# Transforming a long filter with half the rows: taps turned in pairs by half an angle, the skip term moved into tap 0, and 21 weight low parts made by an adding transfer

## The chip, the core and the metric

The kernel runs on one core of a Trainium2 chip. A core has a matrix engine, TensorE (PE in the profile; PEld is its loading of weights), and three engines for everything else: VectorE (DVE), ScalarE (ACT) and GpSimd (POOL). SyncE (SP), ScalarE and GpSimd also issue DMA transfers. Each engine works through its own queue in order, and an instruction waits there until the semaphores that it needs have arrived. The metric is the device time of one execution in microseconds, the median of several runs.

## What is computed

One layer of an encoder on 512 tokens of width 2048: a normalised input is projected; one branch is a Hyena convolution with long two-sided filters (1024 channels), the other an attention; both are gated, added and projected, and a SwiGLU network follows. All is float32. The change touches the Hyena branch alone:

```python
def implicit_filter(...):                 # h: a small network over 512 positions
    h_fwd = h[:, :HYENA_W] * decay
    h_bwd = h[:, HYENA_W:] * decay
    k = jnp.concatenate([h_fwd, jnp.zeros((1, HYENA_W)), h_bwd[:0:-1]], axis=0)
    return k / jnp.sum(jnp.abs(k), axis=0, keepdims=True)

def bidir_fft_conv(u, k):
    uf = jnp.fft.rfft(u, n=2 * L, axis=1)
    kf = jnp.fft.rfft(k, n=2 * L, axis=0)
    return jnp.fft.irfft(uf * kf[None], n=2 * L, axis=1)[:, :L]

    z = hv * x1
    z = bidir_fft_conv(z, filt) + hy_bias * z
    y_h = z * x0
```

The term `hy_bias * z` is called the skip term below. It equals a filter whose tap 0 is larger by `hy_bias`.

## The kernel before

**Products in three parts.** Every float32 operand of a matmul is cut into a high part (rounded, `fp32r`) and a low part (what is left). A product is three matmuls: high by high, high by low, low by high (`mm3`). A group of 512 output columns is one matmul row of 128 x 512.

**Weights.** All weight matrices lie in DRAM as one array `wpk` of tiles of 128 x 1024, in the order of use. `wblk` (L173) hands them out in blocks of 128 columns, 8 to a tile. For each tile SP loads `raw` (two buffers), ScalarE copies it to the high part `wh` and VectorE subtracts to get the low part `wl` (three buffers each; L186 to L188). Tiles 16 to 71 do that with priority, so they stand early in each queue. One block feeds one `mm3` of a projection, 24 matmuls for a tile.

**The Hyena stage** lasts from about 20 to 400 us. The 1024 channels go in four quarters `q` of 256, two tiles of 128 channels each. TensorE runs the projections `px` and `phv` (for `x1`, `hv` and `x0`) without end, and generators put the filter and the convolution between their matmuls: each `yield n` means "go on n steps later", where a step is one block of a projection (three matmuls). They are:

- `taps_gen(q)` (L355): the filter network's last product, times decay, gives forward and backward taps `fd`, `bd`; their absolute sum gives the norm `rn`; `hs`, `hd` are sums and differences of both, even and odd positions apart.
- `filter_gen(q)` (L390): transposes `hs` and `hd` (`ktp`, 16 transposes), splits them into high and low parts (`k...h`, `k...l`), and multiplies them with tables of cosines and sines `CS` of 256 x 256 in two parts (`kp`). The tables are cut in halves of 128 frequencies, `fb` 0 and 1, and 128 taps, `j` 0 and 1. The results are turned by an angle per frequency (`cosw`, `sinw`) into three factors `K` and written to DRAM, to `kd[q]` (POOL's queue).
- `conv_gen(q)` (L435): transposes the signal (`ztp`, split into `zt...h` and `zt...l`), multiplies it with the same tables (`up`), loads the factors back (`kc`, two buffers, POOL's queue), forms the complex products on VectorE (`cu`, `cv`, `Y`), splits them, and transforms back (`ab`). It scales by `rn`, adds the skip term (L504) and multiplies by `x0`.

For each quarter the order is: projections, `conv_gen(q)` queued, `filter_gen(q + 1)` queued; `taps_gen(q + 1)` runs inside `conv_gen(q)`. A scheduler puts the instructions of each engine into one fixed order when the kernel is built. Filter work shares seven buffers (`work`, L286) and eight banks of PSUM.

After this stage come attention, gates, output projection and the feed-forward network, which the change leaves as they are.

Of the kernel before, what the change touches and what calls it, by code (L numbers as in the profile page):

```python
# [11 lines left out]
F32 = mybir.dt.float32  # L12
# [5 lines left out]
P = 128  # L18
S = 512
# [34 lines left out]
W_FIRST = 16, 72  # L54

# [4 lines left out]
for _name, _w in (("mixg", KT), ("ffng", KT), ("bgate", 2 * KT), ("cw", 72), ("cb", 24), ("hyb", HT),  # L60
                  ("cosw", 2), ("sinw", 2), ("nsinw", 2), ("one", 1)):
    PC[_name] = _n
    _n += _w
# [50 lines left out]
def layer_kernel(tc, wpk, xT, par, flt, zemb, w4, decT, tb2, rope, qkg, out):  # L114
# [13 lines left out]
    def ps_tile(name):  # L128
        return banks["pool"].tile([P, S], F32, tag="ps", bufs=banks["n"], name=name)
# [43 lines left out]
    def wblk(nb=1):  # L173
        st = state
        if st["pos"] >= BLK:
            i = st["tile"]
            raw = wpool.tile([P, BLK * P], F32, tag="raw", bufs=2, name=f"wr{i}")
            hi = wpool.tile([P, BLK * P], F32R, tag="whi", bufs=3, name=f"wh{i}")
            lo = wpool.tile([P, BLK * P], F32R, tag="wlo", bufs=3, name=f"wl{i}")
            st.update(tile=i + 1, pos=0, hi=hi, lo=lo, raw=raw)  # L180

        i, n = st["tile"] - 1, {1: XW // 2, 2: XW}.get(st["tile"], BLK)
        if st["pos"] % n == 0:
            c = slice(st["pos"] * P, (st["pos"] + n) * P)
            with tc.high_priority() if W_FIRST[0] <= i < W_FIRST[1] else nullcontext():
                nc.sync.dma_start(st["raw"][:, c], wpk[i, :, c])  # L186
                nc.scalar.copy(st["hi"][:, c], st["raw"][:, c])  # L187
                nc.vector.tensor_tensor(st["lo"][:, c], st["raw"][:, c], st["hi"][:, c].bitcast(F32), ALU.subtract)  # L188
# [43 lines left out]
    prm = cpool.tile([P, NPC + 6], F32, name="prm")[:, :NPC]  # L232
# [53 lines left out]
    def work(name):  # L286
        return cw(name, [P, S], "wk", 7)
# [67 lines left out]
    def taps_gen(q):  # L355
# [3 lines left out]
        for c in range(2):  # L359
# [17 lines left out]
            nc.vector.tensor_tensor(r, n2[:, 0:1], n2[:, 1:2], ALU.add)  # L377
            nc.vector.tensor_scalar(r, r, 256.0, None, ALU.mult)
# [11 lines left out]
    def filter_gen(q):  # L390
# [17 lines left out]
        kd[q] = dpool.tile([256, 6 * 256], F32, tag=f"kd{q}", bufs=1, name=f"kd{q}")  # L408
        for fb in range(2):
            g = []  # L410
            for i in range(2):
                kp = ps_tile(f"kp{q}{fb}{i}")
                for j in range(2):
# [5 lines left out]
            nc.scalar.activation(cr, g[0], AF.Copy, scale=pcol("cosw", fb))  # L419
            nc.scalar.activation(ci, g[1], AF.Copy, scale=pcol("cosw", fb))  # L420
            k1, k2, k3 = (work(f"K{i}{q}{fb}") for i in range(3))
            nc.vector.scalar_tensor_tensor(k1, g[1], pcol("sinw", fb), cr, ALU.mult, ALU.add)
            nc.vector.scalar_tensor_tensor(k2, g[0], pcol("nsinw", fb), ci, ALU.mult, ALU.add)
            nc.vector.scalar_tensor_tensor(k3[:, :256], g[1][:, 256:], pcol("nsinw", fb), cr[:, 256:], ALU.mult, ALU.add)
            nc.vector.scalar_tensor_tensor(k3[:, 256:], g[0][:, 256:], pcol("sinw", fb), ci[:, 256:], ALU.mult, ALU.add)
            rows = kd[q][fb * P:(fb + 1) * P]
# [8 lines left out]
    def conv_gen(q):  # L435
# [61 lines left out]
        for c in range(2):  # L497
# [6 lines left out]
            nc.vector.scalar_tensor_tensor(y, zl[c], pcol("hyb", ct), y, ALU.mult, ALU.add)  # L504
# [844 lines left out]
def _constants():  # L1349
# [33 lines left out]
    return tb2, cosw, sinw, zemb, decT, rope  # L1383


def _arrays(inp):
# [3 lines left out]
    tb2, cosw, sinw, zemb, decT, rope = _constants()  # L1390
# [27 lines left out]
    put("one", np.ones((P, 1), f4))  # L1418

# [28 lines left out]
```

## Time and profile before

| | us |
|---|---|
| median of 3 runs (2510.12 to 2510.76) | 2510.73 |
| the profiled execution | 2510.3 |
| its span, first to last instruction | 2508.5 |
| of which VectorE is busy | 2071.2 |
| of which ScalarE is busy | 1180.0 |

The profile holds one execution. A row of its time line gives the start in us, the duration, the engine, the line of the source, the operation with output and inputs, and in square brackets how long the engine stood idle before and who released it. A row may merge several equal instructions (x2). Matmuls overlap, so the time that one costs is the distance from its start to the next one's start. VectorE and ScalarE rows overlap by about 0.1 us in the same way. In the table of DMA issues the last number is the median time from issue to landing. "Waits" lists who waited for whom, with the total, how often, and the longest.

### The profile page before, as it was taken

How to read it: one execution, taken by the hardware profiler on the slowest of the kernel's cores; microseconds unless marked ns; L12 is line 12 of the kernel's file. 1: busy time of each engine (PE TensorE's matmuls, PEld its weight loads, DVE VectorE, ACT ScalarE, POOL GpSimd, SP SyncE). 2: the span in 40 equal slices, each digit the busy share in tenths (PEclk: the TensorE clock that was granted, in tenths of full speed). 3: DMA queues.
4: the chain of work that ended last, by engine and by line, in shares of the span. 5: the costliest groups of instructions: out<-in, count | busy, mean ns of one | idle time of the engine just before them, and what ended most of it. 6: DMA issues, size and time to landing. Idle time of an engine off the chain costs nothing.

```text
span 2508.5 us, 34437 instructions
## 1 busy us (share of the span) xinstructions
PE 2501.2 (100%) x13162; PEld 2150.4 (86%) x13162; DVE 2071.2 (83%) x2936; ACT 1180.0 (47%) x1755; POOL 177.5 (7%) x287
## 2 busy tenths in 40 slices
PE   9999999999999999999999999999999999999999
PEld 7888888888888888888888888888888888888888
DVE  7799974855579999664999999999999988997988
ACT  6434324554455445443544444444444455445443
POOL 0000002020000000000000000000000002001111
PEclk9999999999999999999999999999999999999999
DMA  6344443223554444554333333333333348557754
GB/s 214 109 137 134 133 145 108 71 97 117 178 176 155 143 154 144 185 176 140 112 117 120 132 112 126 118 121 132 110 134 110 132 137 214 151 146 189 193 154 109
DMA packets 113281, 350.41 MB, mean 140 GB/s; under 512 B 13723, under 2 KB 15003, under 8 KB 112892
## 3 DMA queue, kind: packets, MB, share of 16 engines
q1 hardware_dynamic: 70128, 248.02, 29.8%
q0 software_dynamic: 22576, 63.19, 9.6%
q10 hardware_dynamic: 20412, 37.00, 4.8%
q8 instruction: 103, 1.69, 0.3%
q14 instruction: 62, 0.51, 0.1%
HBM read 297.56 MB, written 54.26 MB: 140 GB/s over the span
## 4 chain that ended last, share of the span: by engine, by line
PE 80%; DVE 1%; ACT 0%; issue 0%; ACTq 0%
PE fx L132 19%; PE fy L132 10%; PE b L132 7%; PE o L132 7%; PE gx L132 6%; PE d L132 5%; PE fz L132 5%; PE dx L132 4%; PE ex L132 3%; PE gy L132 3%; PE dy L132 2%; PE ey L132 2%; PE gz L132 2%; PE q L132 1%; PE dz L132 1%; PE av L132 1%
## 5 line engine op out<-in xcount | busy, mean ns | idle before, releaser
L187 ACT CAST wh<-wr 128x1024 fp32r<-128x1024 f32 (+1 forms) x168 | 173.2, 1031 | 289.3 <-PE o L132 65.9
L188 DVE TENSOR_TENSOR wl<-wr,wh 128x1024 fp32r<-128x1024 f32 (+1 forms) x168 | 201.1, 1197 | 123.0 <-ACT wh L187 122.0
L881 ACT CAST fwhs<-fs 128x1024 fp32r<-128x1024 f32 x176 | 184.7, 1050 | 87.3 <-PE fz L132 68.9
L883 DVE TENSOR_TENSOR fwls<-fs,fwhs 128x1024 fp32r<-128x1024 f32 x176 | 214.6, 1219 | 4.4 <-ACT fwhs L881 4.3
L881 ACT CAST fwha<-fa 128x1024 fp32r<-128x1024 f32 x132 | 138.9, 1053 | 151.5 <-PE fx L132 83.8
L132 PE MATMUL px<-xh,wh 128*128 128x512 f32 x576 | 180.5, 395 | 0.0
L132 PE MATMUL fx<-fX,fwhs 128*128 128x512 f32 x704 | 175.3, 391 | 0.6 <-DVE fv L925 0.6
L132 PE MATMUL fy<-fX,fwhs 128*128 128x512 f32 x704 | 175.4, 391 | 0.0
L132 PE MATMUL fx<-fX,fwha 128*128 128x512 f32 x704 | 172.0, 391 | 0.2 <-DVE c L930 0.2
L883 DVE TENSOR_TENSOR fwla<-fa,fwha 128x1024 fp32r<-128x1024 f32 x132 | 161.4, 1223 | 10.0 <-ACT fwha L881 9.8
L132 PE MATMUL o<-ms,wh 128*128 128x512 f32 x512 | 157.8, 389 | 0.0
L132 PEld LDWEIGHTS fx<-fX,fwhs 128*128 128x128 f32 x704 | 129.3, 188 | 25.7 <-DVE fv L925 0.9
L132 PEld LDWEIGHTS fx<-fX,fwha 128*128 128x128 f32 x704 | 129.3, 188 | 25.4 <-issue 0.6
L132 PEld LDWEIGHTS fy<-fX,fwhs 128*128 128x128 f32 x704 | 129.3, 188 | 24.9
L132 PEld LDWEIGHTS px<-xh,wh 128*128 128x128 f32 x576 | 106.7, 189 | 24.1 <-issue 2.4
L132 PE MATMUL d<-act,wh 128*128 128x512 f32 x384 | 118.3, 389 | 0.0
L132 PEld LDWEIGHTS o<-ms,wh 128*128 128x128 f32 x512 | 96.1, 188 | 19.9
L132 PE MATMUL px<-xh,wl 128*128 128x512 f32 x288 | 113.0, 392 | 0.0
L874 DVE TENSOR_TENSOR fs<-fa,fa 128x1024 f32<-128x1024 f32 x88 | 107.2, 1219 | 1.7 <-PE o L132 1.0
L874 DVE TENSOR_TENSOR fs<-fs,fa 128x1024 f32<-128x1024 f32 x88 | 107.3, 1219 | 1.0 <-PE o L132 0.2
L132 PE MATMUL o<-ms,wl 128*128 128x512 f32 x256 | 99.7, 389 | 0.0
L132 PE MATMUL fy<-fX,fwls 128*128 128x256 f32 x704 | 98.7, 283 | 0.0
(965 smaller groups left out, 5891.0 us busy)
## 6 DMA issues: line engine op xcount, KB each, us to landing
fa<-wpk SPq DMA_DIRECT2D x176, 512.0 KB, 3.9
wr<-wpk SPq DMA_DIRECT2D x162, 512.0 KB, 3.5
ga<-wpk SPq DMA_DIRECT2D x60, 512.0 KB, 3.7
da<-wpk SPq DMA_DIRECT2D x32, 512.0 KB, 3.8
ea<-wpk SPq DMA_DIRECT2D x32, 512.0 KB, 4.2
actd<-c POOLq DMA_DIRECT2D x41, 256.0 KB, 4.2
actr<-actd ACTq DMA_DIRECT2D x41, 256.0 KB, 4.1
kc<-kd POOLq DMA_DIRECT2D x16, 512.0 KB, 4.4
```

Source lines behind the costliest of these rows:

```text
L132: tc.keep_in_program_order(nc.tensor.matmul(out, lhsT=lhsT, rhs=rhs, start=start, stop=stop, **kw))
L187: nc.scalar.copy(st["hi"][:, c], st["raw"][:, c])
L188: nc.vector.tensor_tensor(st["lo"][:, c], st["raw"][:, c], st["hi"][:, c].bitcast(F32), ALU.subtract)
L874: raws["sum"] = nc.vector.tensor_tensor(t, a, b, ALU.add).ins
L881: nc.scalar.copy(hi, w)
L883: raws["wl"] = nc.vector.tensor_tensor(lo, w, hi.bitcast(F32), ALU.subtract).ins
```

## The change

**Half the rows.** The taps belong to a transform with an odd frequency grid. If each tap and its mirror in the upper half are first turned by half an angle, every frequency of the even half is the sum, and every one of the odd half the difference, of the same two results, and these come from one table of 128 x 128 in place of 256 x 256. So `hs` and `hd` are laid out with the upper half mirrored, the transposed taps are turned (`kt`, `kr`, with `cosa`, `sina`) before they are split, and each product `kp` uses one block of the table. The two results of a sum are combined by one more step (`kc` copy and `G`; `inner` masks the first row) into the values of both halves. The halves `fb` are now even and odd frequencies, so the rows of `kd` alternate, and the loads of the second half start one row later and fetch the last row apart (127 rows and 1 row).

**The skip term** is added to tap 0 (one column, times the filter's norm), and the line that added it to the result is gone.

**Low parts by transfer.** For the 21 even tiles from 8 to 48 the low part is no longer VectorE's subtraction. ScalarE writes the negated, rounded tile into `wl`, and a DMA of POOL's queue reads the same tile from DRAM again and adds it.

```diff
+W_FETCH = range(8, 50, 2)
...
                 nc.scalar.copy(st["hi"][:, c], st["raw"][:, c])
-                nc.vector.tensor_tensor(st["lo"][:, c], st["raw"][:, c], st["hi"][:, c].bitcast(F32), ALU.subtract)
+                if i in W_FETCH:
+                    nc.scalar.activation(st["lo"][:, c], st["raw"][:, c], AF.Copy, scale=-1.0)
+                    nc.gpsimd.dma_start(st["lo"][:, c], wpk[i, :, c], accum_op=ALU.add)
+                else:
+                    nc.vector.tensor_tensor(st["lo"][:, c], st["raw"][:, c], st["hi"][:, c].bitcast(F32), ALU.subtract)
...
+            nc.vector.scalar_tensor_tensor(fd[:, :1], r, pcol("hyb", 2 * q + c), fd[:, :1], ALU.mult, ALU.add)
...
+            ahead = fd.rearrange("p (m n) -> p n m", n=2)
+            back = bd[:, 1:].rearrange("p (m n) -> p n m", n=2)[:, ::-1]
             for h, op in ((hs, ALU.add), (hd, ALU.subtract)):
-                nc.vector.tensor_tensor(h[:, :256], fd[:, ::2], bd[:, 2::2], op)
-                nc.vector.tensor_tensor(h[:, 256:], fd[:, 1::2], bd[:, 1:S:2], op)
+                h = h.rearrange("p (n m) -> p n m", n=2)
+                nc.vector.tensor_tensor(h[:, :, :P], ahead[:, :, :P], back[:, :, :P], op)
+                nc.vector.tensor_tensor(h[:, :, P:][:, :, ::-1], ahead[:, :, P:], back[:, :, P:], op)
...
-                taps.append(split(cv, tp, "kh", "kl", 4, 4, f"k{i}{q}{j}"))
+            for j in range(2):
+                t = tmp(f"kt{q}{i}{j}")
+                nc.scalar.activation(t, tps[1 - j], AF.Copy, scale=pcol("sina" if i == j else "nsina"))
+                turned = work(f"kr{q}{i}{j}")
+                nc.vector.scalar_tensor_tensor(turned, tps[j], pcol("cosa"), t, ALU.mult, ALU.add)
+                taps.append(split(cv, turned, "kh", "kl", 4, 4, f"k{i}{q}{j}"))
             yield 3
...
+        for i in range(2):
+            g = [ps_tile(f"kp{q}{i}{w}") for w in range(2)]
+            for w in range(2):
+                mm3(g[w], part(w, 0, 3 * P, 4 * P), part(w, 1, 3 * P, 4 * P), *taps[2 * i + (w ^ i)], True, True)
+            cc = tmp(f"kc{q}{i}")
+            nc.scalar.copy(cc, g[0])
+            for fb, (a, b, op) in enumerate(((g[1], cc, ALU.add), (cc, g[1], ALU.subtract))):
+                spectra[fb].append(work(f"G{q}{fb}{i}"))
+                nc.vector.scalar_tensor_tensor(spectra[fb][i], a, pcol("inner"), b, ALU.mult, op)
+            yield 3
         for fb in range(2):
-            g = []
-            for i in range(2):
-                kp = ps_tile(f"kp{q}{fb}{i}")
-                for j in range(2):
-                    a = j * 256 + fb * P
-                    mm3(kp, part(i, 0, a, a + P), part(i, 1, a, a + P), *taps[2 * i + j], j == 0, j == 1)
-                g.append(kp)
-                yield 2
+            g = spectra[fb]
...
-            rows = kd[q][fb * P:(fb + 1) * P]
+            rows = kd[q].rearrange("(p s) c -> p s c", s=2)[:, 1 - fb]
...
-                nc.gpsimd.dma_start(kc[ph], kd[q][fb * P:(fb + 1) * P, ph * S:ph * S + 2 * S])
+                for p0, r0, n in ((0, 129, P - 1), (P - 1, 0, 1)) if fb else ((0, 1, P),):
+                    nc.gpsimd.dma_start(kc[ph][p0:p0 + n], kd[q][r0:r0 + n, ph * S:ph * S + 2 * S])
...
-            nc.vector.scalar_tensor_tensor(y, zl[c], pcol("hyb", ct), y, ALU.mult, ALU.add)
```

The order in which the instructions stand moves in three places that matter. A row names the line, the operation, output, inputs and shape.

First VectorE's queue in the first quarter, from the filter's factors `K` to the first low part of the transposed signal, `zt00l`, which the convolution's matmul `up000` reads. Before:

```order
L422 SCALAR_TENSOR_TENSOR K000_1073<-kp001_1056,prm_78,kcr00_1069 128x512
L423 SCALAR_TENSOR_TENSOR K100_1074<-kp000_1043,prm_78,kci00_1070 128x512
L424 SCALAR_TENSOR_TENSOR K200_1075<-kp001_1056,prm_78,kcr00_1069 128x256
L188 TENSOR_TENSOR wl20_1234<-wr20_1232,wh20_1233 128x1024
L425 SCALAR_TENSOR_TENSOR K200_1075<-kp000_1043,prm_78,kci00_1070 128x256
L558 TENSOR_TENSOR x13u_1091<-px13_970,rbc_542 128x512
L422 SCALAR_TENSOR_TENSOR K001_1126<-kp011_1109,prm_78,kcr01_1122 128x512
L423 SCALAR_TENSOR_TENSOR K101_1127<-kp010_1083,prm_78,kci01_1123 128x512
L424 SCALAR_TENSOR_TENSOR K201_1128<-kp011_1109,prm_78,kcr01_1122 128x256
L425 SCALAR_TENSOR_TENSOR K201_1128<-kp010_1083,prm_78,kci01_1123 128x256
L209 TENSOR_TENSOR zt00l_1145<-ztp00_1139,zt00h_1144 128x512
```

And now, from the third of the factors on (K000 and K100 stand just ahead):

```order
L444 SCALAR_TENSOR_TENSOR K200_1132<-G001_1099,prm_78,kcr00_1126 128x256
L445 SCALAR_TENSOR_TENSOR K200_1132<-G000_1076,prm_78,kci00_1127 128x256
L442 SCALAR_TENSOR_TENSOR K001_1144<-G011_1101,prm_78,kcr01_1140 128x512
L443 SCALAR_TENSOR_TENSOR K101_1145<-G010_1078,prm_78,kci01_1141 128x512
L580 SCALAR_TENSOR_TENSOR hvo2_973<-hv2u_974,prm_78,hvo2_973 128x511
L444 SCALAR_TENSOR_TENSOR K201_1146<-G011_1101,prm_78,kcr01_1140 128x256
L581 SCALAR_TENSOR_TENSOR hvo2_973<-hv2u_974,prm_78,hvo2_973 128x511
L194 TENSOR_TENSOR wl21_1327<-wr21_1325,wh21_1326 128x1024
L600 TENSOR_TENSOR z2_979<-hvo2_973,x1o2_860 128x512
L445 SCALAR_TENSOR_TENSOR K201_1146<-G010_1078,prm_78,kci01_1141 128x256
L604 TENSOR_TENSOR zf2_981<-z2_979 128x256 x2
L215 TENSOR_TENSOR zt00l_1163<-ztp00_1157,zt00h_1162 128x512
```

Before, the factors of the first half were made while the matmuls of the second half ran; now both sets follow the last of the matmuls, and the short convolution `hvo2`, a weight low part and `z2`, `zf2` have come to stand ahead of `zt00l`.

Second ScalarE's queue at the same place, now: `wl20` is the negated copy for the adding transfer, `kcr` and `kci` are what the factors `K` wait for. Before, a single weight copy stood ahead of each pair.

```order
L430 COPY kc01_1097<-kp010_1089 128x512
L189 CAST wh20_1269<-wr20_1268 128x1024
L191 ACTIVATE wl20_1270<-wr20_1268 128x1024
L439 ACTIVATE kcr00_1126<-G000_1076,prm_78 128x512
L440 ACTIVATE kci00_1127<-G001_1099,prm_78 128x512
L439 ACTIVATE kcr01_1140<-G010_1078,prm_78 128x512
L214 CAST zt00h_1162<-ztp00_1157 128x512
L440 ACTIVATE kci01_1141<-G011_1101,prm_78 128x512
```

So `kcr00` comes behind two copies of a whole weight tile, and all four of `kcr` and `kci` stand after the last spectrum matmul.

Third VectorE's queue at the taps of the second quarter. Before, the low parts of the taps follow the skip term (L504) and the last products of the quarter before:

```order
L504 SCALAR_TENSOR_TENSOR y1_1565<-z1_678,prm_78,y1_1565 128x512
L209 TENSOR_TENSOR k010l_1582<-ktp100_1576,k010h_1581 128x512
L508 TENSOR_TENSOR yh1_750<-yh1_750,y1_1565 128x512
L188 TENSOR_TENSOR wl28_1779<-wr28_1777,wh28_1778 128x1024
L209 TENSOR_TENSOR k011l_1591<-ktp101_1585,k011h_1590 128x512
L209 TENSOR_TENSOR k110l_1609<-ktp110_1603,k110h_1608 128x512
L209 TENSOR_TENSOR k111l_1618<-ktp111_1612,k111h_1617 128x512
```

Now the turnings `kr` stand among them:

```order
L415 SCALAR_TENSOR_TENSOR kr100_1611<-ktp100_1599,prm_78,kt100_1609 128x512
L528 TENSOR_TENSOR yh1_752<-yh1_752,y1_1583 128x512
L377 MEMSET bd20_2008 128x1
L215 TENSOR_TENSOR k010l_1614<-kr100_1611,k010h_1613 128x512
L415 SCALAR_TENSOR_TENSOR kr101_1619<-ktp101_1600,prm_78,kt101_1617 128x512
L415 SCALAR_TENSOR_TENSOR kr110_1646<-ktp110_1634,prm_78,kt110_1644 128x512
L215 TENSOR_TENSOR k011l_1622<-kr101_1619,k011h_1621 128x512
L215 TENSOR_TENSOR k110l_1649<-kr110_1646,k110h_1648 128x512
```

The weight low part `wl28` is gone from this place, since tile 28 is one of the 21, and three turnings stand ahead of `k011l`.

More of the change, by code (lines that the diff above doesn't have):

```diff
@@ L60 @@
 for _name, _w in (("mixg", KT), ("ffng", KT), ("bgate", 2 * KT), ("cw", 72), ("cb", 24), ("hyb", HT),
-                  ("cosw", 2), ("sinw", 2), ("nsinw", 2), ("one", 1)):
+                  ("cosw", 2), ("sinw", 2), ("nsinw", 2), ("one", 1),
+                  ("cosa", 1), ("sina", 1), ("nsina", 1), ("ncosw", 1), ("inner", 1)):
     PC[_name] = _n
@@ L229, in rsqrt @@
         return y
-    prm = cpool.tile([P, NPC + 6], F32, name="prm")[:, :NPC]
+    prm = cpool.tile([P, NPC + 1], F32, name="prm")[:, :NPC]
     nc.scalar.dma_start(prm, par)
@@ L395, in filter_gen @@
         for i, src in enumerate((hs_l, hd_l)):
-            for j in range(2):
-                tp = ps_tile(f"ktp{q}{i}{j}")
+            tps = [ps_tile(f"ktp{q}{i}{j}") for j in range(2)]
+            for j, tp in enumerate(tps):
                 for n in range(4):
@@ L408, in filter_gen @@
         kd[q] = dpool.tile([256, 6 * 256], F32, tag=f"kd{q}", bufs=1, name=f"kd{q}")
-        for fb in range(2):
-            g = []
-            for i in range(2):
-                kp = ps_tile(f"kp{q}{fb}{i}")
-                for j in range(2):
-                    a = j * 256 + fb * P
-                    mm3(kp, part(i, 0, a, a + P), part(i, 1, a, a + P), *taps[2 * i + j], j == 0, j == 1)
-                g.append(kp)
-                yield 2
+        spectra = [], []
+        for i in range(2):
[8 more added lines that the diff above has]
+            yield 3
+        for fb in range(2):
+            g = spectra[fb]
+            sin, nsin = ("sinw", "nsinw")[::1 - 2 * fb]
             cr, ci = tmp(f"kcr{q}{fb}"), tmp(f"kci{q}{fb}")
             nc.scalar.activation(cr, g[0], AF.Copy, scale=pcol("cosw", fb))
-            nc.scalar.activation(ci, g[1], AF.Copy, scale=pcol("cosw", fb))
+            nc.scalar.activation(ci, g[1], AF.Copy, scale=pcol("ncosw" if fb else "cosw"))
             k1, k2, k3 = (work(f"K{i}{q}{fb}") for i in range(3))
-            nc.vector.scalar_tensor_tensor(k1, g[1], pcol("sinw", fb), cr, ALU.mult, ALU.add)
+            nc.vector.scalar_tensor_tensor(k1, g[1], pcol(sin, fb), cr, ALU.mult, ALU.add)
             nc.vector.scalar_tensor_tensor(k2, g[0], pcol("nsinw", fb), ci, ALU.mult, ALU.add)
-            nc.vector.scalar_tensor_tensor(k3[:, :256], g[1][:, 256:], pcol("nsinw", fb), cr[:, 256:], ALU.mult, ALU.add)
+            nc.vector.scalar_tensor_tensor(k3[:, :256], g[1][:, 256:], pcol(nsin, fb), cr[:, 256:], ALU.mult, ALU.add)
             nc.vector.scalar_tensor_tensor(k3[:, 256:], g[0][:, 256:], pcol("sinw", fb), ci[:, 256:], ALU.mult, ALU.add)
-            rows = kd[q][fb * P:(fb + 1) * P]
+            rows = kd[q].rearrange("(p s) c -> p s c", s=2)[:, 1 - fb]
             nc.gpsimd.dma_start(rows[:, :S], k3)
@@ L1359, in _constants @@
     cs = np.stack([np.cos(np.pi * arg / 1024.0), np.sin(np.pi * arg / 1024.0)]).astype(f4)
+    ang = np.pi / 256.0 * (2 * np.arange(P)[:, None] + 1)
+    cs[0, P:, P:] = np.cos(ang * np.arange(P))
+    cs[1, P:, P:] = np.sin(ang * np.where(np.arange(P), np.arange(P), P))
     tb2 = two_part(cs).reshape(2, 2, 2, P, 256).transpose(0, 1, 3, 2, 4).reshape(2, 2, P, S)
-    w = np.pi * (2 * m + 1) / 1024.0
-    cosw, sinw = (t.astype(f4).reshape(2, P).T for t in (np.cos(w), np.sin(w)))
+    w = np.pi * (2 * (np.stack([2 * i[:P], 2 * i[:P] - 1]) % 256) + 1) / 1024.0
+    cosw, sinw = (t.astype(f4).T for t in (np.cos(w), np.sin(w)))
+    ang = np.pi * (2 * i[:P, None] + 1) / 1024.0
+    cosa, sina = np.cos(ang).astype(f4), np.sin(ang).astype(f4)
     pos = np.arange(S, dtype=f4)
@@ L1418, in _arrays @@
     put("one", np.ones((P, 1), f4))
+    put("cosa", cosa)
+    put("sina", sina)
+    put("nsina", -sina)
+    put("ncosw", -cosw[:, 1:])
+    put("inner", (np.arange(P) > 0).astype(f4)[:, None])
     flt = np.zeros((P, 260), f4)
```

4 lines of the change are left out of this document (2 added, 2 removed).

## The prediction, made before the changed kernel had run

> **What bounds the kernel now.** I began with the busy times and the cut into two stretches, because they say on which engine a saving counts.
>
> ```profile
> PE 2501.2 (100%) x13162; PEld 2150.4 (86%) x13162; DVE 2071.2 (83%) x2936; ACT 1180.0 (47%) x1755; POOL 177.5 (7%) x287
> 20.00:400.00 380.00, 380.00 (x1779) 314.03 (x1778) 316.00 (x521) 156.02 (x253) 35.09 (x60) 1.00 0.42 137
> ```
>
> TensorE is busy for all but 7.3 us of the 2508.5 us span, and in the stretch from 20 to 400 us, where everything that is changed runs, it has no hole at all. The clock granted there is 1.00. The waits of TensorE come next, all of them:
>
> ```profile
> PE warm L132 <- DVE wones L245: 1.1, 1, 1.1
> PE fx L132 <- DVE fv L925: 0.6, 1, 0.6
> PE sp L132 <- ACT p L712: 0.5, 2, 0.3
> PE gx L132 <- DVE gX L844: 0.4, 1, 0.4
> PE rs2ss L132 <- DVE acc L278: 0.2, 1, 0.2
> PE fx L132 <- DVE c L930: 0.2, 1, 0.2
> ```
>
> None belongs to the filter or the convolution. So a matmul taken out there shortens the run by its whole step, and so does every new wait lengthen it: nothing else is late, and nothing can be won by making another engine faster. The question is only whether VectorE and ScalarE still deliver in time when the matmuls between two of their jobs are gone.
>
> **What is removed.** The time that a matmul costs is the step from its start to the next one's, not its own length, since they overlap:
>
> ```profile
> 110.58 0.39 PE L132 MATMUL kp<-k000h,CS 128*128 128x512 f32 x1
> ...
> 111.73 0.39 PE L132 MATMUL kp<-k001h,CS 128*128 128x512 f32 x1
> ```
>
> These are the first and the sixth matmul of one group: five steps in 1.15 us, 0.23 us each. Before, a quarter of the channels takes 2 halves x 2 sums x 2 row blocks x 3 parts = 24 of them, now 2 sums x 2 tables x 3 parts = 12. Four quarters save 48 x 0.23 = **11.0 us**. The transposes stay 64, and the order of the other matmuls is the same, so there is no other term on TensorE itself.
>
> **What is added beside it.** Per quarter VectorE gets four turnings of taps (line 415) and four sums (line 433), and loses two skip terms (L504); ScalarE gets six copies. The durations and steps of such instructions stand in this piece of the time line, where one row begins when the one before it lets go:
>
> ```profile
> 121.21 0.75 DVE L422 SCALAR_TENSOR_TENSOR K<-kp,prm,kcr 128x512 f32<-128x512 f32 x1 [1.58 <-ACT kci L420]
> 121.88 0.74 DVE L423 SCALAR_TENSOR_TENSOR K<-kp,prm,kci 128x512 f32<-128x512 f32 x1
> 122.54 0.47 DVE L424 SCALAR_TENSOR_TENSOR K<-kp,prm,kcr 128x256 f32<-128x256 f32 x1
> 122.93 0.47 DVE L425 SCALAR_TENSOR_TENSOR K<-kp,prm,kci 128x256 f32<-128x256 f32 x1
> 123.55 0.69 DVE L209 TENSOR_TENSOR zt00l<-ztp,zt00h 128x512 fp32r<-128x512 f32 x1
> ...
> 126.96 1.22 DVE L188 TENSOR_TENSOR wl<-wr,wh 128x1024 fp32r<-128x1024 f32 x1
> 128.09 0.69 DVE L580 TENSOR_TENSOR z<-hvo,x1o 128x512 f32<-128x512 f32 x1
> 128.70 0.68 DVE L209 TENSOR_TENSOR zt01l<-ztp,zt01h 128x512 fp32r<-128x512 f32 x1
> ...
> 128.92 0.39 PE L132 MATMUL up<-zt00l,CS 128*128 128x512 f32 x1
> ```
>
> A 512-column row with a scalar steps 0.67 us, one of 256 columns 0.39, a weight low part 1.13 (126.96 to 128.09), a plain 512-column row 0.61. VectorE's balance over the stage is 32 x 0.67 - 8 x 0.67 - 21 x 1.13 = -7.7 us: it ends up with less to do. What decides is not the sum but the order in each queue, and I follow it at the places where TensorE can run dry.
>
> **Place A, from filter to convolution in the first quarter.** In the rows above, the low part zt00l is ready at 123.55 + 0.69 = 124.24 us and first used at 128.92: 4.7 us of cover. In the changed order all eight K rows stand together ahead of it, because both halves of the spectrum are done at once. Let T be the start of the last spectrum matmul. TensorE's path: 37 matmuls and 8 transposes lie between it and the matmul that reads zt00l. The transposes step 0.10:
>
> ```profile
> 100.60 1.03 PE L135 MATMUL ktp<-ident,hs 128*128 128x128 f32 x8
> 101.39 0.71 PE L132 MATMUL px<-xh,wh 128*128 128x512 f32 x2
> ```
>
> So TensorE is there at T + 38 x 0.23 + 8 x 0.10 = T + 9.5. ScalarE's path: the high part of weight tile 20 stands ahead of the first kcr, and it waits until the second matmul after T has freed tile 17's buffer, T + 0.46 + 0.39 = T + 0.85. Its step, and so I take it the step of the new negated copy too, is 0.96:
>
> ```profile
> 100.57 1.05 ACT L187 CAST wh<-wr 128x1024 fp32r<-128x1024 f32 x1 [3.25 <-PE phv L132]
> 101.53 0.58 ACT L208 CAST k000h<-ktp 128x512 fp32r<-128x512 f32 x1
> 112.16 0.69 ACT L419 ACTIVATE kcr<-kp,prm 128x512 f32<-128x512 f32 x1 [3.29 <-PE kp L132]
> ```
>
> kcr ends at T + 0.85 + 2 x 0.96 + 0.69 = T + 3.5. VectorE then runs, in this order, K (4 x 0.67, 4 x 0.39), hvo twice (1.34), one weight low part (1.13), z (0.61), zf twice (0.67) and zt00l itself (0.69): 8.7 us, T + 12.2. The wait is **2.7 us**, and for zt01l, which stands one 0.67 row further on, another 0.5: **3.2 us** together. In the later quarters the rows that stand between are fewer, and I see no wait there.
>
> **Place B, the taps of quarters two to four.** Here the cover of before can be read directly, as the end of a low part against its first use:
>
> ```profile
> 177.26 0.68 DVE L209 TENSOR_TENSOR k011l<-ktp,k011h 128x512 fp32r<-128x512 f32 x1
> 179.45 0.39 PE L132 MATMUL kp<-k011l,CS 128*128 128x512 f32 x1
> ...
> 244.08 0.69 DVE L209 TENSOR_TENSOR k021l<-ktp,k021h 128x512 fp32r<-128x512 f32 x1
> 247.38 0.39 PE L132 MATMUL kp<-k021l,CS 128*128 128x512 f32 x1
> ...
> 314.08 0.70 DVE L209 TENSOR_TENSOR k031l<-ktp,k031h 128x512 fp32r<-128x512 f32 x1
> 315.30 0.39 PE L132 MATMUL kp<-k031l,CS 128*128 128x512 f32 x1
> ```
>
> 1.5, 2.6 and 0.5 us. Up to four turnings come before the later low parts (2.7 us), and each high part can only be made once its turning is done, which puts one 0.6 us copy of ScalarE (the k000h row) in the chain: 3.3 us more, less the cover, is 1.8 + 0.7 + 2.8 = 5.3 us. If the two skip rows that go, 1.3 us ahead of this place, are credited in full, it is 0.5 + 0 + 1.5 = 2.0. I take 4.5, nearer to the upper end, since chains across two engines start late, and keep 2.0 to 5.3.
>
> **Place C, the rest of the convolution.** A kc load now waits for all six kd writes of its quarter and no longer for three, as frequencies of both halves share rows, and the folding stands in other places before the transposes. In the fourth quarter no filter work follows that would fill the gap. No row prices this; the nearest are VectorE's one wait for a kc load, of 3.1 us, and TensorE's none. Bounds 0 and 5 us, and I take 2.5, one wait of about that size.
>
> ```profile
>   DVE cu L465: 3.1, 1
> ```
>
> **The adding transfers** of 21 low parts. A weight tile is consumed in 5.49 us, as its copies to high parts show where nothing else runs:
>
> ```profile
> 138.95 1.06 ACT L187 CAST wh<-wr 128x1024 fp32r<-128x1024 f32 x1 [1.01 <-PE px L132]
> 144.44 1.06 ACT L187 CAST wh<-wr 128x1024 fp32r<-128x1024 f32 x1 [4.43 <-PE px L132]
> ```
>
> With three buffers a fetch has two tiles, 11.0 us, plus the two matmuls ahead of the first use of the low part, less 0.4 for the last matmul's end and 2.0 for the two copies: 9.0 us. On POOL's queue no fetch stands behind a write or load that is still waiting when the fetch is ready; the writes and loads behind a fetch wait with it only for the negated copy, which ScalarE makes straight after the high part. SP's next load into the raw buffer waits for that copy instead of VectorE's subtraction, two steps of about 1 us after the buffer is filled either way. How long it takes is not in the trace; the nearest rows are plain and adding transfers from POOL:
>
> ```profile
> kc<-kd POOLq DMA_DIRECT2D x16, 512.0 KB, 4.4
> x2d<-dt POOLq DMA_DIRECT2D x32, 256.0 KB, 5.7
> x2d<-x POOLq DMA_DIRECT2D x16, 256.0 KB, 3.3
> ```
>
> Adding costs 2.4 us more at 256 KB. At 512 KB that makes 4.4 + 2.4 = 6.8, or 9.2 if the extra doubles with the size. I take 7.5 and no wait. If that cover is gone, each microsecond beyond 9 is paid at up to 21 places.
>
> **The sum.** -11.0 + 3.2 + 4.5 + 2.5 = -0.8 us on the profiled execution, which took 2510.3 us with what lies around its span, 0.4 under the median of 2510.73. From that median: **2509.9 us**. With the low ends (3.2 + 2.0 + 0) it is 2504.9, with the high ends (3.2 + 5.3 + 5) 2513.2; place A is a sum of some twenty steps, and a kd write that lands late holds a K buffer there, so I let it go from 1.3 to 10: 2503 to 2520.
>
> **The rivals.** First, **the covers hold**: VectorE's 7.7 us less work brings the low parts forward and nothing waits for long. With at most 3 us of waits it is 2499.7 to 2502.7. For it speaks that TensorE waits nowhere here now; against it the order at place A, which leaves no gap to catch up in.
>
> Second, on the other side, **the short load is carried by one DMA engine**. The second kc load of a half is cut into 127 rows and one row. If 127 rows can't be shared out, one engine moves 127 x 4 KB = 0.52 MB. The rate of one engine follows from this row: 248.02 MB in 0.298 x 16 x 2508.5 us is 20.7 KB per us.
>
> ```profile
> q1 hardware_dynamic: 70128, 248.02, 29.8%
> ```
>
> That is 25 us where it is 4.4 now. VectorE's products wait for it, and with a cover of about 5 us (place A's 4.7) each quarter loses some 16 us: 4 x 16 - 11 + 10 = 63 more, 2574 us. It decides from about 9 us of landing on. The Trainium skill speaks of just this, in "DMA: Bandwidth & Descriptors", section "Why a DMA increments its semaphore by 16 and not by 1": the number of engines is the largest up to 16 that divides both sides' slowest dimension, so 127 partitions get one; but it notes as measured on trn2 that the GpSimd path gives some direct copies all 16 engines with the rows rounded up, 127 among them. By its rule the time is this rival's, by its exception the sum stands; no row of before has such a shape, and since POOL issues this load I lean on the exception.
>
> Third, **the adding transfer lands late**: at 11 us instead of 7.5, about ten of the 21 places lie where no filter work stretches the tile, 10 x 1 to 2 us: 2520 to 2530.
>
> **How the numbers follow.** The forecast, gains and waits about even, gets 0.72 with its own range 2503 to 2520; the covers hold 0.12; one DMA engine 0.07; a late transfer 0.09. A measurement of this kernel tells about 0.2%, 5 us, from no change. Faster than 2505.7: the 0.12 and 0.10 of the forecast's lower part, 0.22. Slower than 2515.8: 0.07 + 0.09 and 0.05 of its upper part, 0.21. Within: 0.57. For 8 in 10 I go from 2502 to 2521, which leaves out most of the first rival, the second and a part of the third.
>
> **What would show it.** The spectrum matmuls should be 48 and step 0.23. TensorE's waits should name zt00l and zt01l (about 3 us), then low and high parts k of quarters two to four, then ab or ktp; if they are missing, the covers held. The 127-row load should land in about 4.5 us, and the fetches in 6.5 to 9; a TensorE wait on a transfer, or VectorE rows cu that wait over 10 us, would make the prediction wrong.

## The result, and the profile after

The changed kernel takes 2534.34 us (median of 6 runs, 2531.43 to 2536.29), the kernel before 2510.4 beside it: a ratio of 1.0094, 95% interval 1.0081 to 1.0107. It is slower by 24 us, and the forecast of 2509.9 with its range of 2502 to 2521 was wrong. The profiled execution took 2536.29 us with a span of 2534.5, 26.0 more than the span before. One execution among all that follow, the profiled one of paced_skip_old, ran at a granted clock of 0.65 from end to end and is left out.

The busy times of the page, and the stretch from 20 to 400 us (columns: sum, busy time of PE, PEld, DVE, ACT, POOL, granted clock, DMA share, GB/s):

```profile
PE 2505.0 (99%) x13114; PEld 2148.7 (85%) x13114; DVE 2065.2 (81%) x2947; ACT 1214.2 (48%) x1800; POOL 201.6 (8%) x316
```

```profile
20.00:400.00 380.00, 357.86 (x1614) 290.50 (x1613) 296.04 (x498) 177.92 (x263) 54.23 (x81) 0.97 0.58 159
```

The 48 matmuls are gone (13162 to 13114) and VectorE is busy for 6.0 us less. But TensorE, without a hole there before, now stands idle for 22.1 us of the stretch, and its clock fell from 1.00 to 0.97. Its waits there, longest first (total, times, longest):

```profile
PE up L134 <- DVE zt00l L215: 5.2, 1, 5.2
PE kv L134 <- DVE x07u L578: 3.5, 1, 3.5
PE ktp L137 <- DVE hs L394: 2.9, 2, 2.3
PE up L134 <- DVE zt20l L215: 1.9, 1, 1.9
PE ab L134 <- ACT Yt311h L214: 1.4, 1, 1.4
...
PE kp L134 <- DVE k131l L215: 1.2, 1, 1.2
PE kp L134 <- DVE k020l L215: 1.2, 1, 1.2
```

None of TensorE's waits names a transfer. The time line of VectorE and TensorE at the longest hole:

```profile
122.03 0.74 DVE L580 SCALAR_TENSOR_TENSOR hvo<-hv2u,prm,hvo 128x511 f32<-128x511 f32 x1
...
124.39 0.40 PE L134 MATMUL up<-zt00h,CS 128*128 128x512 f32 x1
125.36 0.48 DVE L444 SCALAR_TENSOR_TENSOR K<-G,prm,kcr 128x256 f32<-128x256 f32 x1 [2.59 <-DMA kd<-K]
...
129.22 0.68 DVE L215 TENSOR_TENSOR zt00l<-ztp,zt00h 128x512 fp32r<-128x512 f32 x1
...
129.96 0.79 PE L134 MATMUL up<-zt00l,CS 128*128 128x512 f32 x1 [5.17 <-DVE zt00l L215]
...
130.55 0.63 PE L134 MATMUL up<-zt00h,CS 128*128 128x512 f32 x1
...
130.98 0.63 PE L134 MATMUL up<-zt01h,CS 128*128 128x512 f32 x1
```

Two things are to be seen. The seventh K row (the sixth K tile) waits 2.59 us until a kd write has left its buffer, and zt00l stands behind it. And behind the hole matmuls step 0.43 us in place of 0.23. Windows of 2 us over the same place show why (second number in each row: PE busy; the clock is the third from the end):

```profile
126.00:128.00 2.00, 0.00 (x0) 0.00 (x0) 2.00 (x3) 0.00 (x0) 0.00 (x0) 1.00 0.50 199
128.00:130.00 2.00, 0.04 (x1) 0.04 (x1) 2.00 (x6) 0.82 (x1) 0.55 (x1) 0.67 0.67 213
130.00:132.00 2.00, 2.00 (x5) 1.48 (x6) 1.82 (x3) 0.00 (x0) 0.03 (x1) 0.50 0.46 180
132.00:134.00 2.00, 2.00 (x7) 1.52 (x6) 0.00 (x0) 0.00 (x0) 1.06 (x2) 0.50 0.29 53
134.00:136.00 2.00, 2.00 (x7) 1.63 (x6) 0.17 (x1) 0.00 (x0) 0.00 (x0) 0.62 1.00 406
136.00:138.00 2.00, 2.00 (x11) 1.63 (x10) 2.00 (x2) 0.81 (x1) 0.00 (x0) 1.00 0.16 66
```

The clock goes to a half during the hole and stays there until about 135.5 us. Such windows over the whole stage show four more places like this. Time lost while TensorE worked, (1 - clock) times its busy time, is 10.7 us in all.

**The account**: 48 matmuls less, -11.0; holes, +22.1; the tail of the last matmul ahead of each of 17 holes (its 0.39 us less the step of 0.23, hidden before), +2.7; half clock, +10.7. That is +24.5 where the spans differ by 26.0; 1.5 us are not placed.

Last, two waits of VectorE and three rows of the DMA issues (KB, median us to landing):

```profile
DVE cu L486 <- DMA kc<-kd: 21.6, 5, 7.2
...
DVE K L444 <- DMA kd<-K: 4.7, 2, 2.6
```

```profile
wl<-wpk POOLq DMA_DIRECT2D x21, 512.0 KB, 7.7
kd<-K POOLq DMA_DIRECT2D x24, 256.0 KB, 4.3
...
kc<-kd POOLq DMA_DIRECT2D x8, 508.0 KB, 5.5
```

VectorE waited once, 3.1 us, for a kc load before; now it waits five times, 21.6 us. In the fourth quarter the time line shows such a wait reach TensorE, over VectorE's queue:

```profile
350.92 1.11 POOL L475 DMA_DIRECT2D kc<-kd  x2 [8.49 <-DMA kd<-K]
...
354.77 1.22 DVE L486 TENSOR_TENSOR cu<-up,kc 128x1024 f32<-128x1024 f32 x1 [7.22 <-DMA kc<-kd]
355.92 1.21 DVE L487 TENSOR_TENSOR cv<-up,kc 128x1024 f32<-128x1024 f32 x1
357.05 0.68 DVE L578 TENSOR_TENSOR x07u<-px,rbc 128x512 f32<-128x512 f32 x1
...
357.78 0.79 PE L134 MATMUL kv<-wh,xh 128*128 128x512 f32 x1 [3.46 <-DVE x07u L578]
```

POOL's load waits for the last kd write, `cu` waits for the load, `x07u` stands behind `cu` and `cv`, and TensorE's `kv` waits for `x07u`. From 354.77 on VectorE has no pause until it has made Yt311l at 381.4, and there TensorE waits 1.4 us for Yt311h and 0.3 for Yt311l.

### The profile page after: what moved, and what is told of

The parts are those of the page before. It is cut to its first block, busy times and chain, and to the rows that moved or that the text cites. A ratio compares the mean times of both kernels' runs of the same rounds, so it can differ in the third digit from the quotient of the medians.

```text
span 2534.5 us, 34484 instructions
## 1 busy us (share of the span) xinstructions
PE 2505.0 (99%) x13114; PEld 2148.7 (85%) x13114; DVE 2065.2 (81%) x2947; ACT 1214.2 (48%) x1800; POOL 201.6 (8%) x316
## 3 DMA queue, kind: packets, MB, share of 16 engines
q0 software_dynamic: 25856, 74.20, 11.9%
## 4 chain that ended last, share of the span: by engine, by line
PE 79%; DVE 1%; ACT 0%; issue 0%; ACTq 0%
PE fx L134 19%; PE fy L134 10%; PE b L134 7%; PE o L134 7%; PE gx L134 6%; PE d L134 5%; PE fz L134 5%; PE dx L134 4%; PE ex L134 3%; PE gy L134 3%; PE ey L134 2%; PE dy L134 2%; PE gz L134 2%; PE q L134 1%; PE dz L134 1%; PE av L134 1%
## 5 line engine op out<-in xcount | busy, mean ns | idle before, releaser
L194 DVE TENSOR_TENSOR wl<-wr,wh 128x1024 fp32r<-128x1024 f32 (+1 forms) x147 | 175.5, 1194 | 125.8 <-ACT wh L189 125.7
```

## The experiments

Three theories stood at the start. T1: the halved transform makes the holes, by its order and the round trip over kd. T2: the adding transfers make them. T3, beside either: the low clock follows from the holes. T1 was later split into T1a (chains too long for the matmuls over them, which gaps would cure) and T1b (VectorE has too much to do in the stage, so that gaps only move holes).

### One part of the change at a time

transform_only is the changed kernel with `W_FETCH = ()`; fetch_only and skip_only are the kernel before with one part each:

```diff
+                if i in W_FETCH:
+                    nc.scalar.activation(st["lo"][:, c], st["raw"][:, c], AF.Copy, scale=-1.0)
+                    nc.gpsimd.dma_start(st["lo"][:, c], wpk[i, :, c], accum_op=ALU.add)
```

```diff
+            nc.vector.scalar_tensor_tensor(fd[:, :1], r, pcol("hyb", 2 * q + c), fd[:, :1], ALU.mult, ALU.add)
...
-            nc.vector.scalar_tensor_tensor(y, zl[c], pcol("hyb", ct), y, ALU.mult, ALU.add)
```

> The changed kernel without the adding transfers: all low parts are VectorE's subtractions again, the halved transform and the skip term in tap 0 stay. T1 (the new order of the filter and the round trip from kd to kc make TensorE's holes): the holes stay, VectorE even has 21 x 1.13 = 23.7 us more to do in the stage; 2526 to 2545 us, with 15 to 30 us of holes and granted clock below 1.00 behind them. T2 (the adding transfers make the holes, by POOL's queue, their traffic or ScalarE's 21 more copies): the holes go and the 48 matmuls are won, 2499 to 2504 us.

> The kernel before with the adding transfers for the same 21 tiles and nothing else. T1: they are hidden, as their landing of 7.7 us is under the cover of 9 us; 2509 to 2513 us, no new TensorE wait over 0.5 us. T2: most of the 22 us of holes and the 12 us of lost clock come back here, 2530 to 2545 us.

> The kernel before with the skip term in tap 0 and nothing else. It takes eight rows of 0.67 us off VectorE and puts the norm, and ScalarE's two sums of absolute values, ahead of half of hs. In the kernel before hs ends 2.9 and 3.9 us ahead of the transposes that read it (quarters two and four), and the norm follows it by about 1 us. If that cover holds: no wait of ktp for hs over 0.3 us, 2509.5 to 2511.5 us. If the norm's chain is longer than the cover: waits of ktp for hs of 1 to 3 us in three quarters, 2512 to 2520.

| | us | ratio to before, 95% |
|---|---|---|
| transform_only | 2530.0 | 1.0078 [1.0063, 1.0093] |
| fetch_only | 2510.52 | 1.0002 [0.9992, 1.0011] |
| skip_only | 2510.34 | 1.0000 [0.9991, 1.0009] |

All of TensorE's waits from 20 to 430 us in fetch_only are one row; in skip_only there is none:

```profile
PE ab L133 <- DVE Yt311l L214: 0.2, 1, 0.2
```

In transform_only the stage is full of holes (the same columns as above, 380 less 361.4 is 18.6 us, and a clock of 0.98):

```profile
20.00:400.00 380.00, 361.41 (x1639) 291.64 (x1638) 319.46 (x519) 159.18 (x241) 35.61 (x60) 0.98 0.40 130
```

So T2 falls as the main cause: 21 adding transfers alone are hidden, and the transform (with the skip term) alone is slower by 20 of the 24 us. Whether the transfers add the other 4 beside it stays open, since the intervals of transform_only and the whole change overlap. The traces do show that the transfers lengthen the round trip: without them a kd write lands after 3.2 us and not 4.3, VectorE waits 12.0 us for kc loads and not 21.6, no K row waits for a buffer, and the holes before zt00l and `kv` are 3.2 and 0.7 us in place of 5.2 and 3.5. Against that stand other waits, ktp for hs 3.7 in place of 2.9 among them, in 25 holes in place of 17. In fetch_only, too, the median kd write lands after 4.8 us (3.4 before).

### What a hole costs

holes is the kernel before with a transpose behind six groups of the attention's output products, which reads the group's result through a chain of copies; no result uses it:

```diff
+    HOLES = {2: 0, 4: 1, 6: 2, 8: 3, 10: 5, 12: 8}
+    def hole(m, src):
+        uv = [tmp(f"hole{m}{j}") for j in range(2)] if HOLES[m] else []
+        for j in range(HOLES[m]):
+            nc.scalar.copy(uv[j % 2], src)
+            src = uv[j % 2]
+        transpose(ps_tile(f"hole{m}")[:, :P], src[:, :P])
```

> The kernel before with six holes put into TensorE's work in the attention's output products, by a transpose that reads a group's result through a chain of 1, 2, 3, 4, 6 and 9 copies of ScalarE (about 0.55 us each); the transposes' results are used by nothing. Holes of about 0.9, 1.5, 2, 2.6, 3.7 and 5.3 us, 16 us in all, and six matmul tails of 0.17. T3 (a hole itself brings a stretch of about 3.4 us at half clock, 1.7 us each): the holes of over 1 us have it, and the run is 16 + 1 + 5 x 1.7 = 25 us over before, 2533 to 2538 us. If the low clock has a cause of its own in the filter's stage: steps of 0.23 right behind each hole, 2525 to 2529 us.

It took 2550.76 us. The copies had to queue on ScalarE, so the holes came out longer, 29.7 us together. Four of them in the time line, and windows of 3.4 us right behind the first four (PE busy, clock):

```profile
661.53 0.33 PE L135 MATMUL hole<-ident,bt 128*128 128x128 f32 x1 [1.40 <-ACT bt L1068]
...
674.82 0.33 PE L135 MATMUL hole<-ident,hole 128*128 128x128 f32 x1 [2.04 <-ACT hole L1077]
...
690.37 0.33 PE L135 MATMUL hole<-ident,hole 128*128 128x128 f32 x1 [2.69 <-ACT hole L1077]
...
708.02 0.47 PE L135 MATMUL hole<-ident,hole 128*128 128x128 f32 x1 [6.39 <-ACT hole L1077]
```

```profile
661.90:665.30 3.40, 3.40 (x16) 1.00 0.93 338
675.20:678.60 3.40, 3.40 (x9) 0.52 0.90 325
690.70:694.10 3.40, 3.40 (x16) 1.00 1.01 345
708.30:711.70 3.40, 3.40 (x9) 0.50 0.00 0
```

T3 holds, far from the filter, in that the low clock comes with the holes: behind those of 2.04, 6.39, 6.38 and 10.82 us the clock is a half, 1.7 to 2.7 us lost each time, 9.0 together. Behind 1.40 and 2.69 it isn't, so length alone does not decide, and the expected half clock behind every hole of over 1 us did not come. Account: 29.7 + 6 x 0.16 for tails + 6 x 0.1 for the transposes + 9.0 = 40.3, and the spans differ by 40.3. In fetch_only and skip_only, with one hole of 0.2 us and none, the clock is 1.00.

### Moving the work apart

Nothing is removed or added in these; the generators only pause longer. conv_later_6 and conv_later_12 raise the earliest start of each convolution (`Z_WAIT0` 16 to 22 and 28, and 10 to 16 and 22 for the later quarters). The gap kernels put pauses at the filter's own ends:

```diff
-        yield 6
+        yield (6, 12, 12, 12)[q]            # gap_taps, gap_both
...
         filt[q] = rn
+        if q == 0: yield 8                  # gap_first_quarter
+        yield (8, 4, 4, 1)[q]               # gap_both
```

> The changed kernel with the convolution of each quarter started 6 steps (6 x 3 x 0.23 = 4.1 us of projection) later. T1 with late operands as the cause: the hole before zt00l (5.2 us) shrinks to about 1 and that before zt20l (1.9) goes, with them up to 6 us of lost clock; what follows in a quarter is pushed 4.1 us towards its end. 2520 to 2531 us. If instead the total of VectorE's work between the projections is what lacks, the holes only move on to k, ab and kv: 2531 to 2540. T2: unchanged, 2531 to 2538.

> The same with 12 steps (8.3 us). T1 with late operands: both holes before zt gone, but the end of the fourth quarter, behind which no projections are left, moves 8 us on, so that its last holes grow by 0 to 8 us; 2518 to 2535 us. T3 beside it in all four runs: wherever a hole of over 1 us stands, the matmul steps behind it go to 0.43 us for about 3.4 us, and where there are no holes the granted clock is 1.00 in every stretch; if the clock is low where no hole precedes it, T3 falls and the clock is a cause of its own.

> The changed kernel with eight more steps (8 x 0.69 = 5.5 us of projection) between the last spectrum product of the first quarter and the transposes of its signal; nothing is removed or added. T1a (the chain from spectrum to first use of zt00l is too long for the matmuls that lie over it): the holes before zt00l go, with them their lost clock: 5.2 + 0.2 + 3, so about 2526 us, 2521 to 2530. T1b (VectorE simply has too much to do in the stage): the hole only moves behind, 2531 to 2540.

> The changed kernel with 12 steps in place of 6 between the transposes of the taps and the first spectrum product in the quarters two to four. T1a: the eight waits of kp for k high and low parts (4.2 us) go, with the clock lost behind them (about 3 us) and what of the fourth quarter they push; the holes before zt00l stay. 2522 to 2530. T1b: 2531 to 2540.

> Both, and 4 steps at the end of the filter in the quarters two and three too. T1a: next to no hole is left in the filter's stage, the clock there is 1.00, and the 48 matmuls are won: 2510.4 - 11.0 + 0 to 5 for holes at the stage's end that move into the key and query transposes: 2499 to 2505 us. T1b: not under 2515.

| | us | ratio, 95% | first-quarter zt00l | k of quarters 2 to 4 | largest new wait |
|---|---|---|---|---|---|
| conv_later_6 | 2532.65 | 1.0087 [1.0072, 1.0102] | 7.0 | 4.2 (after: 4.0) | none |
| conv_later_12 | 2525.38 | 1.0063 [1.0046, 1.0080] | 5.2 | 4.6 | none |
| gap_first_quarter | 2532.81 | 1.0088 [1.0073, 1.0104] | none | 4.7 | up for zt10l 4.1 |
| gap_taps | 2525.67 | 1.0058 [1.0042, 1.0075] | 5.2 | none | up for zt10l 7.2 |
| gap_both | 2524.77 | 1.0055 [1.0040, 1.0070] | none | none | px for wl 9.9 |

The conv_later kernels missed their aim: in the first quarter the convolution starts when filter_gen(0) has ended, which is later than any of these limits, so zt00l still waits. conv_later_12 fell in the range of T1, but for another reason: what it won in holes (16.6 us in place of 22.1) stands at the fourth quarter's end, where the waits of kv (3.5) and of ab for Yt311h (1.4) are gone; with them went 7 of the 10.7 us of half clock. How much half clock a hole brings also differs from one execution to the next of the same kernel: the four of conv_later_6 took 2528.04, 2531.48, 2533.82 and 2535.56 us at mean granted clocks of 0.999, 0.997, 0.996 and 0.995. Each gap removed just the holes it was aimed at, as T1a says, but others came in their place, as T1b says; gap_taps came out in T1a's range, gap_first_quarter and gap_both in T1b's; gap_both gave back 10 of the 24 us where T1a had promised some 30. What it waits for now:

```profile
PE px L134 <- DMA wl<-wpk: 9.9, 3, 5.7
PE kT0p L137 <- issue: 2.2, 1, 2.2
PE kT0p L137 <- DVE ko L693: 1.9, 3, 0.9
```

The chain behind the 5.66 us one, in the time line of POOL, VectorE, ScalarE and TensorE:

```profile
282.58 1.08 POOL L476 DMA_DIRECT2D kc<-kd  x2 [3.14 <-DMA kd<-K]
...
290.58 1.23 DVE L487 TENSOR_TENSOR cu<-up,kc 128x1024 f32<-128x1024 f32 x1 [7.75 <-DMA kc<-kd]
...
295.03 0.62 ACT L214 CAST Yt200h<-Y 128x512 fp32r<-128x512 f32 x1 [14.71 <-DVE Y L492]
...
295.56 1.05 ACT L189 CAST wh<-wr 128x1024 fp32r<-128x1024 f32 x1
...
296.51 1.05 ACT L191 ACTIVATE wl<-wr 128x1024 fp32r<-128x1024 f32 x1
...
297.86 0.91 POOL L192 DMA_DIRECT2D wl<-wpk  x1 [3.58 <-ACT wl L191]
...
305.67 0.79 PE L134 MATMUL px<-xh,wl 128*128 128x512 f32 x1 [5.66 <-DMA wl<-wpk]
```

The kc load waits for the last kd write, VectorE for the load, ScalarE for VectorE's Y; the weight's copies stand behind that Y in ScalarE's queue, the fetch behind the copy, and 7.8 us later TensorE gets its low part. Place C's round trip has reached the weights. The other two rows are the key's transposes: the fourth quarter now ends behind the key projection, and what VectorE makes for these transposes (ko) comes too late.

### The round trip, the transfers and the skip term in the paced kernel

sync_only and gap_both_sync issue the kd writes from SP (`nc.sync.dma_start(rows...)` in place of `nc.gpsimd`), gap_both_nofetch has `W_FETCH = ()`, gap_both_fewer leaves tiles 22, 24 and 44 to VectorE.

> The changed kernel with nothing but its kd writes moved to SP's queue, no gaps. The round trip from kd to kc shortens by one or two us in each quarter, K's waits for a buffer by as much; the chain from spectrum to zt00l stays. If the round trip in POOL's queue is the main cause of the holes: 2515 to 2522. If it is the length of the chains over ScalarE and VectorE (T1a): 2526 to 2534.

> The kernel gap_both with the six kd writes of each quarter issued by SP in place of POOL. In gap_both what is left are three waits of TensorE for a fetched low part (9.9 us), whose transfers stood in POOL's queue behind kc loads, and these behind kd writes. Theory Q (one in-order queue of POOL carries kd writes, kc loads and fetches, and each holds the next): with 24 writes taken off it the fetches leave in time, the three waits go with most of the clock lost behind them (about 4 us): 2508 to 2514 us. Rival L (the fetch and the kc load are slow as transfers, whatever the queue): the waits stay, 2521 to 2527; SP's weight loads, now behind the K factors, may even come later.

> The kernel gap_both without the adding transfers. Its waits for fetched low parts (9.9 us and about 4 of lost clock) go; VectorE gets 21 x 1.13 = 23.7 us more. If the gaps are enough for VectorE with all its low parts: 2506 to 2512 us. If the gaps only work because the fetches make room on VectorE: new waits of ktp for hs and of ab for Yt, 8 to 14 us of them, 2515 to 2526 us.

> The kernel gap_both with 18 adding transfers in place of 21: tiles 22, 24 and 44, whose low parts TensorE waited for, are VectorE's again. Theory Q and rival L agree that these three waits go. If no other fetch takes their place: 2510 to 2516 us; if the next tiles are late in their turn (the queue is full, not these three): 2517 to 2525.

2528.6 (1.0076 [1.0061, 1.0091]), 2520.51 (1.0040 [1.0025, 1.0055]), 2518.85 (1.0036 [1.0022, 1.0051]) and 2521.27 (1.0044 [1.0028, 1.0055]). The queue of the writes is not the main cause: sync_only keeps the holes, and its interval overlaps that of the changed kernel; in gap_both_sync the waits for wl only shrink from 9.9 to 7.4, nearer to rival L than to Q. Without transfers, or with three fewer, the waits for wl are gone and ktp waits for hs instead (4.9 and 4.4 us), less than the 8 to 14 us expected without transfers; with three fewer, no other fetch is late, and the time still fell in the range given for that.

paced joins gaps and kd writes on SP's queue and sizes each gap, so that the fourth quarter ends in time. paced_nofetch is the same with `W_FETCH = ()`, paced_skip_old with the skip term as before, paced_3 and paced_2 have other gaps (the numbers are in their expectations):

```diff
-        yield 6
+        yield (6, 9, 12, 7)[q]
...
-            nc.gpsimd.dma_start(rows[:, :S], k3)
+            nc.sync.dma_start(rows[:, :S], k3)
...
         filt[q] = rn
+        yield (7, 8, 3, 2)[q]
...
-        yield 8 if q + 1 < NQ else 14
+        yield (8, 10, 6, 12)[q]
```

> The changed kernel with all 21 adding transfers, the kd writes on SP's queue, and gaps measured out for each quarter: 7, 8, 3 and 2 steps behind the last spectrum product, 6, 9, 12 and 7 ahead of the first, 8, 10, 6 and 12 ahead of the inverse transform, so that the last quarter ends before the key projection does (in gap_both it ended two steps after it, and the key's transposes then waited 4 us). If order and queues are all that stood against the change: holes of 2 to 7 us left, the clock near 1.00, 2502 to 2509 us. If the longer chains have a price that gaps can't hide, because a gap in one quarter is taken from the next: 2513 to 2522.

> The kernel paced without the adding transfers. If the transfers make the room on VectorE that the gaps need: VectorE has 23.7 us more, holes of 10 to 20 us, 2513 to 2524 us. If the transfers bring nothing: within 3 us of paced, or faster by the waits on them.

> A second set of gaps with fewer transfers: 10, 4, 2 and 4 steps behind the spectrum, 6, 12, 11 and 8 ahead of it, 8, 8, 10 and 12 ahead of the inverse transform, kd writes on SP's queue, tiles 22 and 44 split by VectorE. It ends the last quarter two steps after the key projection again. If the end of the last quarter decides: 3 to 8 us over paced, 2508 to 2515, with the waits of kT0p as in gap_both. If the earlier quarters decide: level with paced or faster.

> The kernel paced with four gaps shifted: 7, 9, 3 and 5 steps behind the last spectrum product, 6, 9, 10 and 6 ahead of the first. If the 8 us of holes left in paced come from single gaps that are too short: 4 to 6 us of holes, 2505 to 2510 us. If VectorE's order follows the new gaps and opens others, level with paced: 2510 to 2514.

> The kernel paced with the skip term as before, a row of VectorE at the end of each channel tile, and the taps without it. If the norm ahead of hs makes the waits of ktp for hs (3.7 us in paced): these shrink to 0 to 1 us; the eight rows of 0.67 us come back in VectorE's queue ahead of the next taps and give 1 to 4 us to k or ab. 2508 to 2514 us. If VectorE's load of that moment makes them: the waits stay or grow, 2513 to 2520.

| | us | ratio, 95% |
|---|---|---|
| paced | 2512.31 | 1.0008 [0.9999, 1.0017] |
| paced_nofetch | 2511.35 | 1.0004 [0.9995, 1.0013] |
| paced_3 | 2514.86 | 1.0017 [1.0008, 1.0026] |
| paced_2 | 2520.1 | 1.0042 [1.0028, 1.0055] |
| paced_skip_old | 2522.83 | 1.0045 [1.0030, 1.0061] |

paced, in the stretch of above and by its two largest waits:

```profile
20.00:400.00 380.00, 371.71 (x1719) 303.55 (x1718) 310.39 (x530) 190.04 (x297) 41.85 (x65) 1.00 0.60 165
```

```profile
PE ktp L137 <- DVE hs L394: 3.7, 2, 2.2
PE px L134 <- DMA wl<-wpk: 2.9, 2, 2.5
```

With all the work of the change, 22 of the 24 us are back: holes of 8.3 us are left in place of 22.1, and half clock follows one of them. Order and timing, not the amount of work, made the loss; how much of the 22 us is due to the gaps and how much to the queue was not separated. But the 11 us are not won either: -11.0 + 8.3 + 1.5 for tails + 1.7 of clock makes 0.5, where the spans differ by 2.0 (what the rest is was not found). paced (2512.31) lies between the two ranges expected, nearer to the second. Shifting single gaps (paced_3) opens others. paced_2 ends late again and the key's transposes wait 5.8 us. The transfers bring nothing even here: paced_nofetch is within 3 us of paced, as the second branch of its expectation says. With the skip term's eight rows back on VectorE the kernel is 10 us slower, outside both ranges expected, so the wait of hs for the norm, which I suspected, is not a net loss here. But the gaps were sized for paced, and where the 10 us stand is not shown; in the kernel before, the skip term in tap 0 changed nothing (skip_only). No version beats the kernel before.

## Why the prediction was wrong

The step that failed is the price of the waits. The prediction added 10.2 us of them to the gain of 11.0; the changed kernel had 22.1, most of the excess at place C. And it put nothing down for what a hole brings beside its length, half clock and matmul tails, 13.4 us more: with every wait right and these left out, the sum would still have been 2521.8.

- **The gain, 11.0 us**: right, 48 matmuls at 0.23.
- **Place A**, 3.2 us: 5.2. The chain came as worked out, beside the 2.59 us for a K buffer held by a kd write, which the prediction named as a reason for a wide range and left out of the sum: 2.7 + 2.59 is, to 0.1 us, the hole of 5.2. These writes were slower than in transform_only (4.3 us against 3.2), where no K row waited and the hole was 3.2; that the adding transfers would slow the other transfers was no term of the prediction. The 0.5 for zt01l did not come: at half clock TensorE was late too.
- **Place A in later quarters**, "I see no wait there": wrong, zt20l cost 1.9. Ahead of it, too, a K row waited for a buffer held by a kd write, 2.15 us.
- **Place B**, 4.5 us: right within its bounds, 4.0 in seven waits, all for k low and high parts of quarters two to four, k131l and k020l longest.
- **Place C**, 2.5 us with bounds 0 and 5: the wait that was mis-sized, 10.9 (kv 3.5, ktp for hs 2.9, ab 4.5). It was priced by the nearest row, one wait of VectorE of 3.1 us, as a single event. But the round trip over kd recurs in each quarter (21.6 us of VectorE's waiting), and it holds up what stands behind it in the in-order queues. For kv the rows at 350 to 358 us show it, and in gap_both it reached the weights; that Yt311h was late by the same backlog is inferred. The hs waits have a further cause: ahead of the longer one (2.3) VectorE waits 2.10 us for the decay table, whose one buffer is loaded only when the tile before has been multiplied.
- **The clock** was missing from the sum. The prediction read 1.00 in the stretch and took it as given, while its own forecast put holes there. It cost 10.7 us, as much as the gain won. The tails of 2.7 were missing too.
- **The covers hold** (0.12) fell with the first row of the waits. **One DMA engine** (0.07) did not happen: 5.5 us for 508 KB against 25. The exception that the Trainium skill notes in "DMA: Bandwidth & Descriptors", section "Why a DMA increments its semaphore by 16 and not by 1", agrees with that. **The adding transfer lands late** (0.09): 7.7 us against the 7.5 taken, and TensorE waited for none in the changed kernel; such waits only appeared in the kernels with gaps, and the one followed up, in gap_both, came from a fetch that itself left late.
- **The chances**: slower had 0.21, from a late transfer and one DMA engine, neither of which happened. That several short waits add up and some cost more than their length was no rival at all.

## What to carry to other kernels

Where an engine runs without a hole, a change that halves its work in a burst also halves the cover of every chain that starts or ends there; write down each chain's length (here two alternating steps of ScalarE and VectorE more at the taps and two at the spectrum, and one DRAM round trip waiting for six writes rather than three) against the matmuls left over it, before counting the saving. As an estimate from these runs, price a TensorE hole at its length plus 0.16 us, and plan for 1.7 us or more of half clock behind any of about 2 us, in one piece or two: holes of 2.04 and of 1.18 with 0.58 us had it, some single ones up to 2.69 did not. If the work is right but the timing wrong, spacing it out by a few numbers gets most back, but only to the length of the stage: each gap is paid by what comes later.

## What the runs showed of the hardware

The clock fell behind short holes, and not behind each of them. It was halved behind one of 2.04 us, and behind 1.18 and 0.58 us close together in the changed kernel (at 254 us, clock 0.50 from 256 to 258), but not behind single ones of 2.69 and 1.87. In paced_3 it stayed at 1.00 behind 14 holes, the longest of 2.4 us. The time lost is the same again and again: (1 - clock) summed over windows of 2 us, idle time counted in, comes to 11.9, 6.8, 8.5, 5.1, 3.4 and 1.7 us in the kernels after, transform_only, gap_both, conv_later_12, gap_both_nofetch and paced, all multiples of 1.7.

The Trainium skill ("TensorE: Matmul & The Clock Gate", section "Why this matters for your kernels") advises against idle gaps of over about 3 us; by these runs that is not short enough. Part 1 of the same page of the Trainium skill speaks of a free-running window of 3413 ns. The trace agrees in that half of it is the 1.7 us above; that the place of a hole in such a window decides beside its length would fit the runs, but no run here shows it directly.
